# Where the preparation of w_out, the weights of FoX and the first loads of the output products stand in a hybrid decoder layer

## The chip, the cores and the metric

One core of a Trainium2 chip runs the program. The metric is device time in microseconds, from the first to the last instruction of the core and the little that lies around them; lower is better.

The engines are named as in the profile: PE (TensorE, with PEld for its weight loads), DVE (VectorE), ACT (ScalarE), POOL (GpSimd) and SP (SyncE), which issues all transfers here. SPq rows are issues of transfers. Each engine works through its instructions in order.

## The reference

A layer of a decoder: RMSNorm, one input projection, three mixers side by side (forgetting attention FoX with 8 heads of 64, gated linear attention GLA, a gated linear recurrence RG-LRU), each gated by silu, one output projection, RMSNorm, residual. 2048 frames and 16 meta tokens, width 1024.

```
hn   = rms_norm(h, pre_g)                      # (2176, 1024), the first 112 rows empty
proj = hn @ w_in                               # all mixers' columns
y    = concat(fox(...) * silu(fg), gla(...) * silu(gg), lru(...) * silu(lg)) * vmask   # width 2048
h    = h + rms_norm(y @ w_out, post_g)         # w_out: 2048 x 1024
return h[:, PAD:]

# FoX: c = cumsum(log_sigmoid(ff + b_f))
s = q.k / sqrt(64) + c[t] - c[s],  causal;   o = softmax(s) @ v
```

## The kernel before

Each float32 product is made of float16 products: a matrix is split into a high and a low half, scaled by a power of two that its sum of squares gives, and three products of halves are added. So every weight passes through a preparation: a load, a square with a sum on ACT, a column sum on PE, some small DVE operations for the scale, then the high half on ACT and the low half on DVE.

The work is a list of jobs (`hybrid_kernel`). Of each job its main part (`mix`) is written out step by step, and between its steps stand those of the next job's preparation (`prep`), which hold the input projections. The jobs are GLA's, then RG-LRU's, then FoX's sixteen. FoX goes by pairs of heads p = 0 to 3 and by chunks c = 0 to 3 of 512 queries; job (p, c) in this text is `fox_attend(k, p, c)`, beside which `fox_prepare` of the following (p, c) runs. A job has 4c + 5 steps, 176 in all.

One step of `fox_attend` takes 128 keys for both heads: eight matmuls into the double bank `sq` (line 1264), of which there is one; the exponential on ACT (line 1272) into `pt`; the sums `za` of the exponentials on DVE and, for one head of every second step, on POOL (line 1280); and two steps later four matmuls with the values (line 1288). At the end ACT copies the sums out (line 1294), and a chain of small transfers through DRAM (lines 503 to 510 and 1306) brings the reciprocals back. `fox_prepare` makes keys, queries, values and gate of its job and the row maxima: query-key products (line 1204), on DVE a maximum (line 1212), then a transposition, three small operations and six small transfers `QA<-dr` (line 1235), which the first step of the job needs.

`post` runs at the start of a job: it ends the conversions that are pending (`load_end`) and begins up to two weights of the list `todo`: `load_begin` issues the load and writes the square (line 454) at once. FoX's weights for pair p + 1 are begun in job (p, 1), keys and values, and in job (p, 3), queries and gate.

`wout_ready` prepares w_out during FoX: 32 blocks are loaded and squared (line 1338), three loads ahead; then in eight groups four blocks each are loaded again, four differences taken on POOL (line 1360), and seven pieces halved (`halves`, lines 1424 and 1425) and stored to DRAM (`wD`, line 1366): 56 halves. These are 95 steps of a generator; `merge` takes one of them behind each step of FoX from job (0, 0) on.

`project_out` then forms y @ w_out by blocks of two 128-row tiles (a pair), seven products of 24 matmuls each (line 1553). A pair's y is loaded (line 1437), squared (line 454 with `junk`), scaled and halved (lines 1468 to 1481, 1424, 1425). The prepared blocks come from `wD` into the memory of the normalised input `xhl` (four blocks, sixteen transfers) and into `ts` (three blocks). `out_begin` does the first pair's loads and halves and the blocks of `xhl` beside job (3, 3).

A scheduler puts the instructions into each engine's order by its own model of their durations. `tc.issue_after(i)` is the program's hold on it: what is written inside is queued behind instruction i on i's engine. `k.mark` and `k.store` name such instructions: the last store of y, of FoX or of w_out's pieces.

Of the kernel before, what the change touches and what calls it, by code (L numbers as in the profile page):

```python
# [11 lines left out]
BF16 = mybir.dt.bfloat16  # L12
# [62 lines left out]

OB = 8
GAP = 2
FA0 = (0, 0, 1, 3, 4, 5)  # L80
FA1 = (0, 0, 3, 5, 8, 9)
# [67 lines left out]
def drain(g):  # L149
    for _ in g:  # L150
        pass
# [15 lines left out]
def hybrid_kernel(tc, xT, x, w_grp, w_fa, vecs, w_a2, w_r, w_i, w_out, post_g, masks, out, yD=None):  # L167
    nc = tc.nc
    with ExitStack() as es:
# [40 lines left out]
        for t in range(8):  # L210
            for c in range(len(LP)):
                load = {}
                if t < 7:
                    load = {(t, 0): [("lx", t + 1), ("lg", t + 1)]}
                else:
                    load = {(7, 0): [("fk", 0), ("fv", 0)], (7, 2): [("fq", 0), ("fg", 0)]}
                flush = (5 * t + c) % 2 == 1
                prep, mix = lru_project(k, t, c), lru_mix(k, t, c, flush)
                if (t, c) == (0, 1):

                    w, prep0, mix0, n0, n_fill = jobs.pop()
                    jobs.append((w, chain(prep0, prep), chain(mix0, mix), n0 + 4, n_fill + 6))
                else:
                    jobs.append((load.get((t, c), []), prep, mix, 4 if flush else 3, 6))
        fox0 = len(jobs)
        for p in range(4):
            for c in range(NCH):
                load = {}
                if p < 3:
                    load = {1: [("fk", p + 1), ("fv", p + 1)], 3: [("fq", p + 1), ("fg", p + 1)]}  # L230
                jobs.append((load.get(c, []), fox_prepare(k, p, c), fox_attend(k, p, c), 4 * c + 5,
                             FILL[c] if (p, c) != (3, 3) else LAST_FILL))
        side = wout_ready(k)
        drain(jobs[0][1])
        for i, (_, _, mix, n_main, _) in enumerate(jobs):
            if i + 1 < len(jobs):
# [173 lines left out]
def load_begin(k, nm):  # L410
    load_dma(k, nm)
    load_squares(k)


def load_dma(k, nm):
    cols, src = (48, k.ins["w_fa"]) if nm == "fa" else (P, k.ins["w_grp"][GROUPS[nm]])
    raw = k.wp.tile([P, KT, P], F32, name="raw", bufs=RAWB)[:, :, 0:cols]
    with k.tc.issue_after(k.mark) if k.mark is not None else nullcontext():
        k.nc.sync.dma_start(out=raw, in_=src)
    k.sent.append((nm, raw, cols))  # L420

# [20 lines left out]
def post(k, n=1):  # L442

    while k.begun:
        load_end(k)
    for _ in range(min(n, len(k.todo))):
        load_begin(k, k.todo.pop(0))


def squares(k, tiles, scale=1.0):  # L450
# [446 lines left out]
        gla_keyed(k, 0, c1)  # L897


def beside(main, side, at):  # L900

    for i, _ in enumerate(main):
        for _ in range(at.count(i)):
            next(side, None)
        yield
# [266 lines left out]
def fox_prepare(k, p, c):  # L1172
# [59 lines left out]
    nc.vector.tensor_tensor(dr[:, 2, :], mr, dr[:, 1, :], op=ALU.subtract)  # L1232
    for h in range(2):
        for t in range(3):
            k.mark = nc.sync.dma_start(out=qx[64 * h + t:64 * h + t + 1, :].rearrange("o (i q) -> o i q", q=P),
                                       in_=dr[4 * h:4 * h + 4, t, :]).ins

    yield from rest
# [4 lines left out]
def fox_attend(k, p, c):  # L1243
# [8 lines left out]
    for j in range(nj):  # L1252
# [13 lines left out]
        if d >= 0:  # L1266
            v0 = NM if d == 0 else 0
            v1 = NM if d == 4 else P
            for h in range(2):
                nc.tensor.matmul(out=sp[0:m, h, off:off + v1 - v0], lhsT=k.identb[0:m, 0:m],  # L1270
                                 rhs=k.trib[0:m, v0:v1], start=False, stop=True)
        nc.scalar.activation(pt[0:m, :, off:], sp[0:m, :, off:], AF.Exp, scale=K.esc[0:m])  # L1272
        for h in range(2):
            if j == 1:
                if off:
# [42 lines left out]
def wout_ready(k):  # L1318
# [11 lines left out]
        return k.wk.tile([P, 2, KT // 2, P], F16, name="ws", tag="WS", bufs=BUFS["WS"])  # L1330

    order = [(q, b, j) for q in range(4) for b in range(4) for j in range(2)]
    raws = [load(*x) for x in order[0:3]]
    yield
    for i, (q, b, j) in enumerate(order):
        if b == j == 0:
            ss = small(k, "ssw", [P, 8], bufs=1)
        nc.scalar.activation(stage()[:, 0].bitcast(BF16), raws.pop(0), AF.Square, scale=2.0,
                             accum_out=ss[:, 2 * b + j:2 * b + j + 1])
        if i + 3 < len(order):  # L1340
            raws.append(load(*order[i + 3]))
        if (b, j) == (3, 1):
            yield
            nc.vector.tensor_reduce(ss[:, 0:1], ss, axis=AX.X, op=ALU.add)
            sc, inv = scale_of(k, ss[:, 0:1])
            for ring, x in ((k.wsc, sc), (k.winvs, inv)):
                ring.append(carve(k, 1))
                nc.vector.tensor_copy(ring[-1], x)
        yield
# [3 lines left out]
    for i, (q, j) in enumerate(groups):  # L1353
# [8 lines left out]

        def put(nm, x):
            hl = stage()
            halves(k, x, k.wsc[q], hl[:, 0], hl[:, 1])
            k.mark = nc.sync.dma_start(out=k.wD[BLOCKS.index(nm), :, j, :, q].rearrange(
                "z p k n -> p z k n"), in_=hl).ins

# [30 lines left out]
def out_begin(k):  # L1399

    nc = k.nc
    k.W = {}
    n = 4 * KT // 2 * P
    views = [[k.xhl[:, (4 * i + z) * n:(4 * i + z + 1) * n].rearrange("p (q k n) -> p q k n", q=4, n=P)
              for z in range(4)] for i in range(4)]
    k.winv = k.xhl[:, 16 * n:16 * n + 2 * CH].bitcast(F32)
    wout_load(k, BLOCKS[0], views[0])
    raws = pair_load(k, 0)
    for i in range(1, 4):
        k.load = wout_load(k, BLOCKS[i], views[i])  # L1410
    for q in range(4):
        nc.gpsimd.tensor_scalar(out=k.winv[:, P * q:P * q + P], in0=k.ones, scalar1=k.winvs[q], scalar2=None,
                                op0=ALU.mult)
    yield
    yield
    k.pairs = pair_halves(k, 0, raws)
    for _ in range(5):
        next(k.pairs)
        yield


# [10 lines left out]
def y_load(k, t):  # L1432
    yv = k.yD.rearrange("(h t p) n -> h p t n", p=P, h=2)
    raws = [tile4(k, "ZZ", "y") for _ in range(2)]
    for h in range(2):
        with k.tc.issue_after(k.store):
            k.load = k.nc.sync.dma_start(out=raws[h], in_=yv[h, :, :, P * t:P * t + P]).ins  # L1437
    return raws

# [184 lines left out]
```

## Time and profile before

| | |
|---|---|
| time, median of 3 runs | 2070.82 us (2068.61 to 2078.42) |
| profiled execution | 2072.19 us, span 2070.5 us |
| PE, DVE, ACT, POOL busy | 1918.2, 1284.5, 1011.7, 641.6 us |
| mean granted clock of PE | 0.968 |
| transferred | 152.70 MB |

The profile comes from one execution. Busy times add up over stages with different limits, so the stretches below are read one by one. A waiting time in brackets is the idle time of that engine just before the instruction, with what ended it. A granted clock of 1.00 is 2.4 GHz, 0.50 would be 1.2 GHz throughout; a number between them says in what share of the stretch each held.

### The profile page before, as it was taken

The numbers are of one execution on the slowest core, as the hardware profiler recorded it, in microseconds if no ns is written. First come the engines' busy times: TensorE is split into PE (matmuls) and PEld (weight loads), VectorE is DVE, ScalarE is ACT, GpSimd is POOL, SyncE is SP. The second block draws the span as 40 slices with busy tenths as digits, with TensorE's granted clock in tenths as the row PEclk, the third lists the DMA queues.
The fourth block names the chain that finished last, engine by engine and source line by source line (L and its number), as shares of the span: only waits on it lengthen the run. The fifth ranks groups of instructions, "written<-read, shape, count | busy, mean of one in ns | idle before, by whom it ended". The sixth has DMA issues, their size and how long they took to land. (4 is left out here: it accounts for less than half of the span.)

```text
span 2070.5 us, 39449 instructions
## 1 busy us (share of the span) xinstructions
PE 1918.2 (93%) x15988; PEld 990.9 (48%) x15988; DVE 1284.5 (62%) x2802; ACT 1011.7 (49%) x1561; POOL 641.6 (31%) x596
## 2 busy tenths in 40 slices
PE   6889999999899999999997989999999997899998
PEld 5455666665455555554333433354335432344443
DVE  6665453445777777754658867534753566487674
ACT  7645642345778888842445533322332235344441
POOL 3434233222333333321125621111211123253432
PEclk9889999999999999999998999999999998999999
DMA  6200120201111111111236640201020006843411
GB/s 220 68 7 28 40 84 27 72 23 51 57 41 41 41 46 42 62 51 29 67 100 205 207 127 12 72 13 32 18 66 12 12 12 234 242 141 96 135 58 61
DMA packets 116135, 152.70 MB, mean 74 GB/s; under 512 B 18792, under 2 KB 75816, under 8 KB 115952
## 3 DMA queue, kind: packets, MB, share of 16 engines
q1 hardware_dynamic: 115952, 150.18, 22.8%
q8 instruction: 125, 2.05, 0.4%
q14 instruction: 58, 0.48, 0.1%
HBM read 108.71 MB, written 41.33 MB: 72 GB/s over the span
## 5 line engine op out<-in xcount | busy, mean ns | idle before, releaser
L480 PE MATMUL pj<-xhl,whl 128*128 128x512 f16 (+3 forms) x3960 | 809.6, 356 | 9.1 <-ACT whl L437 4.2
L480 PEld LDWEIGHTS <-whl 128*128 128x128 f16 x3984 | 364.9, 98 | 391.2 <-issue 68.7
L1272 ACT ACTIVATE pt<-sq,consts 128x1024 f32<-128x1024 f32 (+4 forms) x176 | 163.1, 927 | 263.1 <-PE sq L1270 124.0
L1280 POOL TENSOR_TENSOR za<-za,pt 128x512 f32<-128x512 f32 (+1 forms) x80 | 98.6, 1233 | 540.5 <-ACT pt L1272 491.1
L1212 DVE CUSTOM_DVE_ANT_0 mj<-mq,CB 128x512 bf16<-128x512 f32 (+4 forms) x344 | 189.6, 580 | 69.0 <-PE mq L1204 35.8
L492 PEld LDWEIGHTS <-xhl 128*128 128x128 f16 (+1 forms) x3264 | 193.1, 100 | 35.5 <-issue 30.7
L1553 PEld LDWEIGHTS <-whl 128*128 128x128 f16 x1344 | 131.0, 98 | 164.4 <-issue 8.1
L492 PE MATMUL pj<-whl,xhl 128*128 128x128 f16 (+1 forms) x3024 | 198.1, 224 | 1.1 <-DVE consts L1212 1.1
L1280 DVE TENSOR_TENSOR za<-za,pt 128x512 f32<-128x512 f32 (+3 forms) x208 | 135.5, 675 | 92.0 <-ACT pt L1272 91.1
L1288 PE MATMUL fv<-pt,fv 128*64 128x512 f32 (+4 forms) x704 | 187.4, 549 | 2.1 <-ACT pt L1272 1.9
L1553 PE MATMUL pj<-xhl,whl 128*128 128x512 f16 x768 | 169.1, 380 | 0.0
L1264 PE MATMUL sq<-QA,KA 64*128 64x512 f16 (+4 forms) x1032 | 131.7, 351 | 18.7 <-ACT pt L1272 12.6
L1553 PE MATMUL pj<-ts,whl 128*128 128x512 f16 x576 | 127.9, 383 | 0.0
L558 DVE SCALAR_TENSOR_TENSOR xc<-lx,consts,xc 128x448 f32<-128x448 f32 (+1 forms) x120 | 98.9, 824 | 3.4
L1537 POOL TENSOR_TENSOR o<-o,xt 128x512 f32<-128x512 f32 x31 | 52.6, 1713 | 117.7 <-issue 60.6
L1264 PEld LDWEIGHTS <-KA 64*128 64x128 f16 (+1 forms) x1032 | 41.6, 95 | 95.1 <-issue 69.5
L1204 PE MATMUL mq<-KA,QA 64*128 64x512 f16 (+4 forms) x344 | 61.4, 345 | 21.8 <-DVE consts L1212 20.8
L516 ACT ACTIVATE gate<-pj,consts 128x512 f32<-128x512 f32 (+2 forms) x72 | 46.0, 640 | 72.7 <-PE pj L480 60.2
L1519 ACT ACTIVATE sqo<-o 128x512 bf16<-128x512 f32 x32 | 20.1, 629 | 123.4 <-DVE o L1513 123.4
L1559 DVE SCALAR_TENSOR_TENSOR o<-pj,consts,o 128x512 f32<-128x512 f32 x56 | 41.1, 745 | 59.1 <-PE pj L1553 54.8
L1264 PE MATMUL sq<-QA,KX 64*128 64x512 bf16 (+4 forms) x344 | 68.7, 351 | 3.9 <-DMA QA<-dr 3.9
L517 DVE SCALAR_TENSOR_TENSOR gate<-gate,pj 128x512 f32<-128x512 f32 (+2 forms) x72 | 45.2, 628 | 43.2 <-ACT gate L516 41.7
(253 smaller groups left out, 2832.6 us busy)
## 6 DMA issues: line engine op xcount, KB each, us to landing
raw<-in_w_grp_dram SPq DMA_DIRECT2D x44, 512.0 KB
wr<-in_w_out_dram SPq DMA_DIRECT2D x64, 256.0 KB
y<-yD SPq DMA_DIRECT2D x32, 512.0 KB
wD<-ws SPq DMA_DIRECT2D x56, 256.0 KB
CB<-c32D SPq DMA_DIRECT2D x32, 256.0 KB
xhl<-wD SPq DMA_DIRECT2D x16, 512.0 KB
xt<-in_x_dram SPq DMA_DIRECT2D x16, 512.0 KB
out_dram<-o SPq DMA_DIRECT2D x32, 256.0 KB
```

What stands on the lines that cost most here:

```text
L480: nc.tensor.matmul(out=ps, lhsT=a[:, kt, 0:m], rhs=b[:, kt, u0:u0 + n], start=i == 0, stop=i == 23)
L492: nc.tensor.matmul(out=ps, lhsT=a[:, kt, u0:u0 + m], rhs=b[:, kt, :], start=i == 0, stop=i == 23)
L516: k.act = nc.scalar.activation(out, ps, AF.Tanh, scale=hinv).ins
L558: nc.vector.scalar_tensor_tensor(out=xc, in0=lx[:, j:j + n], scalar=cw(j), in1=xc, op0=ALU.mult, op1=ALU.add)
L1204: nc.tensor.matmul(out=ps[:, h, 0:n], lhsT=qh[hs, P * i:P * i + P], rhs=d.hi[pc][hs, 0:n], start=True, stop=pc < c)
L1212: nc.vector.tensor_tensor_reduce(out=junk[:, h, 0:n], in0=ps[:, h, 0:n], in1=d.cb[pc][:, h, 0:n], scale=1.0, scalar=-3e38, op0=ALU.add, op ...
L1264: nc.tensor.matmul(out=sp[0:m, h, off:], lhsT=a[j // 4][hs, kk], rhs=b[hs, off:], start=i == 0, stop=i == 3 and d < 0)
L1272: nc.scalar.activation(pt[0:m, :, off:], sp[0:m, :, off:], AF.Exp, scale=K.esc[0:m])
L1280: eng.tensor_tensor(out=za[h][0:m, off:], in0=za[h][0:m, off:], in1=pt[0:m, h, off:], op=ALU.add)
L1288: nc.tensor.matmul(out=pv[hs, off1:], lhsT=V1[0:m1, j1 % 4, hs], rhs=pt1[0:m1, h, off1:], start=j1 == 0, stop=j1 == nj - 1)
L1537: eng.tensor_tensor(out=o, in0=o, in1=xt[:, h, :], op=ALU.add)
L1553: nc.tensor.matmul(out=ps, lhsT=a[:, kt, :], rhs=w[b + kt // 4][:, :, kt % 4, :], start=kt + j == 0, stop=(kt, j) == (KT - 1, 2))
```

## The change

- w_out's preparation: its 95 steps are spread over 150 of FoX's steps (`slowed`); its squares and the ACT part of its halves are queued behind the exponential written last (`k.exp`); its loads run six ahead.
- FoX's weights: the load and the square are two entries of `todo` now (`fox_loads`): keys and values are loaded in job (p, 0) and squared in (p, 1), queries and gate loaded in (p, 2) and squared in (p, 3); for pair 0 the same in RG-LRU's last jobs. Loads of other weights are no longer queued behind a store.
- The output: `out_begin` loads y of the first pair and then the blocks behind the last transfer of the maxima's rows (`k.dr`); later pairs' y is queued behind `k.mark`, not behind FoX's last store. The steps beside job (3, 3) are 16, nine of them empty, and the halves are queued behind exponentials.

The same instructions are issued; only their order differs.

```diff
-OB = 8
+OB = 16
+WOUT = (95, 150)
...
-                    load = {(7, 0): [("fk", 0), ("fv", 0)], (7, 2): [("fq", 0), ("fg", 0)]}
+                    load = {(7, c): x for c, x in fox_loads(0).items()}
...
-                load = {}
-                if p < 3:
-                    load = {1: [("fk", p + 1), ("fv", p + 1)], 3: [("fq", p + 1), ("fg", p + 1)]}
+                load = fox_loads(p + 1) if p < 3 else {}
...
-        side = wout_ready(k)
+        side = slowed(wout_ready(k), *WOUT)
...
 def load_dma(k, nm):
-    with k.tc.issue_after(k.mark) if k.mark is not None else nullcontext():
+    with k.tc.issue_after(k.mark) if nm[0] in ("fk", "fv", "fq", "fg") else nullcontext():
         k.nc.sync.dma_start(out=raw, in_=src)
...
     for _ in range(min(n, len(k.todo))):
-        load_begin(k, k.todo.pop(0))
+        nm = k.todo.pop(0)
+        if nm is None:
+            load_squares(k)
+        elif nm[0] == "load":
+            load_dma(k, nm[1])
+        else:
+            load_begin(k, nm)
+
+def fox_loads(p):
+    return {0: [("load", ("fk", p)), ("load", ("fv", p))], 1: [None, None],
+            2: [("load", ("fq", p)), ("load", ("fg", p))], 3: [None, None]}
...
+def slowed(g, n, of):
+    for i in range(of):
+        if (i + 1) * n // of > i * n // of:
+            next(g, None)
+        yield
+    drain(g)
...
-            k.mark = nc.sync.dma_start(out=qx[64 * h + t:64 * h + t + 1, :].rearrange("o (i q) -> o i q", q=P),
+            k.dr = k.mark = nc.sync.dma_start(out=qx[64 * h + t:64 * h + t + 1, :].rearrange("o (i q) -> o i q", q=P),
...
-        nc.scalar.activation(pt[0:m, :, off:], sp[0:m, :, off:], AF.Exp, scale=K.esc[0:m])
+        k.exp = nc.scalar.activation(pt[0:m, :, off:], sp[0:m, :, off:], AF.Exp, scale=K.esc[0:m]).ins
...
-    raws = [load(*x) for x in order[0:3]]
+    raws = [load(*x) for x in order[0:6]]
...
-        nc.scalar.activation(stage()[:, 0].bitcast(BF16), raws.pop(0), AF.Square, scale=2.0,
-                             accum_out=ss[:, 2 * b + j:2 * b + j + 1])
-        if i + 3 < len(order):
-            raws.append(load(*order[i + 3]))
+        with k.tc.issue_after(k.exp):
+            nc.scalar.activation(stage()[:, 0].bitcast(BF16), raws.pop(0), AF.Square, scale=2.0,
+                                 accum_out=ss[:, 2 * b + j:2 * b + j + 1])
+        if i + 6 < len(order):
+            raws.append(load(*order[i + 6]))
...
-            halves(k, x, k.wsc[q], hl[:, 0], hl[:, 1])
+            with k.tc.issue_after(k.exp):
+                halves(k, x, k.wsc[q], hl[:, 0], hl[:, 1])
...
 def out_begin(k):
+    k.mark = k.dr
...
-    wout_load(k, BLOCKS[0], views[0])
     raws = pair_load(k, 0)
-    for i in range(1, 4):
+    for i in range(4):
         k.load = wout_load(k, BLOCKS[i], views[i])
...
-    yield
-    yield
+    for _ in range(9):
+        yield
     k.pairs = pair_halves(k, 0, raws)
     for _ in range(5):
-        next(k.pairs)
+        with k.tc.issue_after(k.exp):
+            next(k.pairs)
         yield
...
-        with k.tc.issue_after(k.store):
+        with k.tc.issue_after(k.mark):
             k.load = k.nc.sync.dma_start(out=raws[h], in_=yv[h, :, :, P * t:P * t + P]).ins
```

Lines of the changed kernel have other numbers (the exponential 1272 is 1292, ACT's half 1424 is 1447, y's square 454 is 465, y's load 1437 is 1460). ACT in the middle of w_out's halves, before (`pt` is an exponential, `ws` a half, `fv` the values of the next job):

```order
L1424 ACTIVATE ws_13677<-wt_13506,consts_58 128x512
L1272 ACTIVATE pt_12968<-sq_12967,consts_58 128x1024
L1424 ACTIVATE ws_13776<-wt_13675,consts_58 128x512
L1424 ACTIVATE ws_13821<-wr_13044,consts_58 128x512
L1158 ACTIVATE fv_12816<-pj_12817,consts_58 128x512
L1424 ACTIVATE ws_13869<-wt_13774,consts_58 128x512
L1272 ACTIVATE pt_13024<-sq_13023,consts_58 128x1024
```

and where the halves begin after the change, in job (1, 2) instead of (0, 3):

```order
L1447 ACTIVATE ws_14309<-wr_14224,consts_58 128x512
L1292 ACTIVATE pt_14379<-sq_14378,consts_58 128x1024
L1447 ACTIVATE ws_14395<-wt_14307,consts_58 128x512
L1292 ACTIVATE pt_14414<-sq_14413,consts_58 128x1024
L1447 ACTIVATE ws_14428<-wr_14228,consts_58 128x512
L1292 ACTIVATE pt_14449<-sq_14448,consts_58 128x1024
L1292 ACTIVATE pt_14478<-sq_14477,consts_58 128x1024
```

Two or three halves between exponentials have become one or none. ACT in job (3, 3), before (`junk<-y` is y's square, `whl` its halves):

```order
L501 COPY zs<-fx 128x512
L1272 ACTIVATE pt<-sq,consts 128x1024 x5
L454 ACTIVATE junk,consts<-y 128x1024
L1272 ACTIVATE pt<-sq,consts 128x1024
L454 ACTIVATE junk,consts<-y 128x1024 x2
L1272 ACTIVATE pt<-sq,consts 128x1024
L454 ACTIVATE junk,consts<-y 128x1024
```

and after:

```order
L512 COPY zs<-fx 128x512
L1292 ACTIVATE pt<-sq,consts 128x1024 x10
L465 ACTIVATE junk,consts<-y 128x1024 x2
L1292 ACTIVATE pt<-sq,consts 128x1024
L465 ACTIVATE junk,consts<-y 128x1024 x2
L1292 ACTIVATE pt<-sq,consts 128x1024
```

The squares moved from behind the fifth exponential to behind the tenth. SP's queue at the start of job (3, 3), before (from the maxima's rows to the first blocks):

```order
L1235 DMA QA<-dr 1x4x128 x6
L503 DMA rowD<-zs 1x512 x2
L505 DMA consts<-rowD 128x8
L510 DMA rowD<-consts 128x8
L1306 DMA rz<-rowD 64x512 x2
L1308 DMA yD<-fo 128x512
L1437 DMA y<-yD 128x8x128 x4
L1394 DMA xhl<-wD 128x2048 x6
```

and after:

```order
L1255 DMA QA<-dr 1x4x128 x6
L1460 DMA y<-yD 128x8x128 x3
L514 DMA rowD<-zs 1x512 x2
L1460 DMA y<-yD 128x8x128
L1416 DMA xhl<-wD 128x2048
L516 DMA consts<-rowD 128x8
L1416 DMA xhl<-wD 128x2048 x2
L521 DMA rowD<-consts 128x8
```

Three of y's four loads now stand ahead of the whole normalisation of job (3, 2), and y's rest and the first blocks between its transfers.

## Rows read from the trace of the kernel before

**Rows 1.** Stretches: length; busy time of each engine; granted TensorE clock; DMA share; GB/s.

```profile
500.00:900.00 400.00, 384.28 (x2128) 220.70 (x2127) 305.40 (x537) 317.80 (x443) 152.99 (x187) 1.00 0.14 46
951.97:1152.80 200.83, 177.06 (x1205) 70.91 (x1204) 133.05 (x349) 90.37 (x153) 64.46 (x44) 0.94 0.36 116
951.97:1057.84 105.87, 98.78 (x663) 37.90 (x662) 63.43 (x207) 43.70 (x80) 17.90 (x15) 0.97 0.21 68
1152.80:1371.72 218.92, 201.12 (x1441) 86.41 (x1440) 142.37 (x356) 83.50 (x115) 63.28 (x49) 0.97 0.30 87
1399.41:1575.42 176.01, 168.16 (x1201) 68.39 (x1200) 97.10 (x293) 58.77 (x76) 31.93 (x25) 0.99 0.13 34
1399.41:1499.82 100.41, 95.89 (x658) 37.36 (x657) 62.17 (x191) 32.06 (x43) 17.53 (x14) 0.98 0.09 24
1399.41:1449.93 50.52, 47.79 (x338) 20.11 (x337) 24.56 (x79) 14.29 (x21) 7.29 (x6) 0.97 0.12 33
1603.10:1649.66 46.56, 46.45 (x338) 19.93 (x337) 24.18 (x76) 11.99 (x16) 7.27 (x6) 1.00 0.04 13
1698.37:1762.81 64.44, 49.76 (x268) 14.45 (x268) 40.45 (x60) 30.10 (x36) 23.38 (x14) 0.84 0.55 195
1762.81:1810.00 47.19, 39.85 (x178) 17.24 (x179) 17.93 (x26) 15.70 (x25) 11.59 (x5) 0.93 0.82 247
```

**Rows 2.** Line 1294: count, duration (min/median/max, ns), first and last start.

```profile
L1294 ACT COPY fo<-fv x16: 566/585/586, 952.0 to 1762.8; 128x512 f32<-128x512 f32 x16
```

**Rows 3.** Timeline of one step of job (3, 3).

```profile
1719.95 0.82 PE L1264 MATMUL sq<-QA,KA 64*128 64x512 f16 x6 [0.19 <-ACT pt L1272]
1720.59 0.39 PE L1264 MATMUL sq<-QA,KX 64*128 64x512 bf16 x2
1721.08 1.11 ACT L1272 ACTIVATE pt<-sq,consts 128x1024 f32<-128x1024 f32 x1 [1.18 <-PE sq L1264]
```

**Rows 4.** Lines of w_out's pieces; L1338 from 951.97 to 1057.84 only.

```profile
L1338 ACT ACTIVATE ws<-wr x19: 612/618/630, 986.2 to 1045.5; 128x512 bf16<-128x512 f32 x19
...
L1424 ACT ACTIVATE ws<-wt,consts x32: 705/712/724, 1101.5 to 1229.0; 128x512 f16<-128x512 f32 x32
...
L1425 DVE SCALAR_TENSOR_TENSOR ws<-wt,consts,ws x32: 732/752/1764, 1107.9 to 1230.3; 128x512 f16<-128x512 f32 x32
...
L1360 POOL TENSOR_TENSOR wt<-wr x16: 1257/1714/5558, 1097.4 to 1217.3; 128x512 f32<-128x512 f32 x16
```

**Rows 5.** ACT's waits, 900 to 1700: total us, times, longest.

```profile
ACT whl L454 <- DMA raw<-in_w_grp_dram: 23.9, 8, 4.4
```

**Rows 6.** Timeline, job (2, 1): start, us, engine, line, operation [idle before, releaser].

```profile
1431.00 1.06 ACT L454 ACTIVATE whl<-raw 128x1024 bf16<-128x1024 f32 x1 [3.76 <-DMA raw<-in_w_grp_dram]
1432.18 0.16 DVE L465 CAST consts<-consts 128x1 bf16<-128x1 f32 x1 [3.62 <-ACT whl L454]
1432.85 1.37 PE L1264 MATMUL sq<-QA,KA 64*128 64x512 f16 x6 [2.62 <-DVE consts L1212]
```

**Rows 7.** Timeline of SP's queue, the end of FoX.

```profile
1705.52 3.78 SPq L1235 DMA_DIRECT2D QA<-dr  x6
1721.18 4.51 SPq L1437 DMA_DIRECT2D y<-yD  x4
1783.24 11.17 SPq L1437 DMA_DIRECT2D y<-yD  x7
```

**Rows 8.** Timeline of ACT, job (3, 3).

```profile
1725.86 1.06 ACT L454 ACTIVATE junk<-y 128x1024 bf16<-128x1024 f32 x1 [3.67 <-DMA y<-yD]
1740.66 1.15 ACT L1424 ACTIVATE whl<-y,consts 128x1024 f16<-128x1024 f32 x1 [5.87 <-DVE consts L320]
```

**Rows 9.** Timeline of TensorE, job (3, 3) and behind.

```profile
1728.06 1.47 PE L1264 MATMUL sq<-QA,KA 64*128 64x512 f16 x6 [3.77 <-ACT pt L1272]
1738.72 0.25 PE L467 MATMUL mx<-consts 128*128 128x1 bf16 x4 [4.13 <-DVE consts L465]
1800.57 0.27 PE L467 MATMUL mx<-consts 128*128 128x1 bf16 x4 [7.34 <-DVE consts L465]
```

## The prediction

> **What bounds the kernel now.** I read the table of stretches first, because the chain that ended last is almost all matmuls of the output products and says little about the stage that the change touches. Its edges are the moments at which a FoX job (p, c) copies its sums out (line 1294, sixteen times) [rows 1, 2]. In each stretch the reader compares TensorE's busy time with the length: the difference is idle, and a granted clock under 1.00 is time at 1.2 instead of 2.4 GHz. Head pair 2's jobs 1 to 3 take 176.01 us with 7.9 idle at 0.99; the same jobs of pair 0 take 200.83 with 23.8 idle at 0.94; pair 1's four jobs take 218.92 with 17.8 idle at 0.97, pair 2's four (1371.72 to 1575.42) 203.70 [rows 1]. These three differ by w_out's preparation alone, which runs beside pairs 0 and 1. Pair 3's job 1, with neither w_out nor weights to load, takes 46.56 us with 0.1 idle; pair 2's job 1, which loads weights, 50.52 with 2.7 idle [rows 1]. The last job (64.44 us, 14.7 idle, clock 0.84) and what follows (47.19, 7.3 idle, 0.93) are the other poor stretches. So TensorE bounds the kernel, and what can be gained is its idle and half-speed time there.
>
> Then the timelines, to see who makes TensorE idle. In FoX's step a query-key product of eight matmuls (0.82 and 0.39 us) must follow the exponential that empties its bank (1.11 us on ACT), and the next exponential follows the product; ACT idles 1.18 us meanwhile [rows 3]. What stands on ACT behind an exponential costs nothing up to 1.2 us; what is above that is added to the step, unless TensorE has projection matmuls left.
>
> **w_out's preparation, 88 pieces on ACT.** Each of 32 squares takes 0.62 us there, each of 56 halves 0.71; a half also takes 0.75 on VectorE, and 32 of them (four in each of eight groups) need a subtraction of some 1.7 us on GpSimd [rows 4]. Nothing is removed; today they stand two, three or up to five between exponentials, later mostly one, queued behind an exponential, over 150 steps instead of 95 of 176. The present price is (200.83 - 176.01) + (218.92 - 203.70) = 40.0 us. Of it 5.5 (105.87 - 100.41) fall on the jobs with 19 squares [rows 1, 4], 0.29 each, though they stand four together; 40.0 - 5.5 = 34.5 over 56 halves is 0.62 each. After the change one piece of 0.62 or 0.71 fits into the 1.2 us, so ACT costs nothing; what remains is VectorE, which the maxima and the sums of FoX share. It is busy 97 of 176 us in the clean jobs, and 56 halves add 42 us (more where GpSimd interferes) spread over some 400. Bounds for a half are 0 and 0.62. I take 0.27, near the squares' 0.29, the nearest row with a single crowded engine: 56 x 0.27 = 15, and 1 for the squares: 16 remain, **24 gained** (bounds 0 to 40).
>
> VectorE's half takes 732 ns at least and 1764 at most; the longest is one subtraction's time above the shortest [rows 4]. The Trainium skill, "SBUF — State Buffer", section "Who interferes with whom", says that a VectorE instruction with two SBUF inputs and a GpSimd instruction that reads SBUF block one another for the whole instruction; the trace agrees in size. By that, spreading moves 32 such collisions beside more maxima of pairs 2 and 3 without making them fewer; the sum by the rule alone would keep the 40 us, and it is priced as two rivals below, from rows.
>
> The moved pieces bring their transfers along: w_out's loads (six ahead instead of three) and stores stand on SP's queue between FoX's small transfers. In the new order each store's VectorE half stands before the maxima's last operation, so no row of maxima waits for it; cost 0, else inside the bounds above.
>
> **FoX's weights.** ACT's square waited for its weights eight times, 23.9 us [rows 5]. The place in pair 2's job 1 shows the chain: square 3.76 us late, VectorE's cast behind it 3.62, TensorE 2.62 because the maxima stand behind that cast [rows 6]. A pair of loads costs 50.52 - 46.56 = 4.0 us, and six such pairs lie within FoX's jobs, 24 us. With the transfer issued a job (28 to 76 us) ahead the wait goes. Late next: two squares of 1.06 us between exponentials, 2.1 against 1.2, so 0.9 and some rest stay, say 1.5 per pair: **15 gained** (bounds 6 and 24). The loads pass the attention's small transfers on SP, and the four buffers are free then, since pending conversions are ended before new loads start. LRU's loads lose their place behind the y stores and move ahead; there TensorE is busy 384 of 400 us [rows 1] and covers them: 0, bounds -4 and +4, a quarter of its idle time there.
>
> **The last job.** y was issued at 1721.18, behind the normalisation of job (3, 2); its first square stood before the sixth exponential, waited 3.67 us, and TensorE idled 3.77; then 4.13 at the scale, the conversion on ACT 5.87 [rows 7 to 9]. Now y is issued right behind the maxima's row (its six small transfers are issued from 1705.52, 3.78 us long), about 11 us earlier, and squared after the tenth exponential, some 20 us after its issue. So these 7.9 us go. In their place: twice two squares, 2 x (2.1 - 1.2) = 1.8; then the scale and two conversions before an exponential, about 3: 4.8 back, 3.1 net. The clock of 0.84 is worth at most 10.3 us (0.16 x 64.44); with shorter gaps I count a fifth, 2.1. **5 gained** (bounds -5 and 14). The wait for the maxima's row itself, at the job's start, stays. GpSimd's sum and VectorE's difference of y now stand at the third step and hold their queues until y lands; their sums of exponentials run two or three buffers behind, which covers it. The normalisation of (3, 2) is overtaken by y and some blocks, but its result is read only by the fifth pair.
>
> **The second pair.** Its y was issued at 1783.24, behind the last store, though it reads rows of chunk 0 only; TensorE idled 7.34 us at 1800.57 [rows 7, 9], and the clock of 0.93 costs at most 0.07 x 47.19 = 3.3 [rows 1]. Now it follows the blocks, at about 1760, while the scale is wanted some four products later: **9 gained** (bounds 0 and 10.6).
>
> Sum: 24 + 15 + 5 + 9 = 53. The profiled execution took 2072.2 us (1.4 above the median of 2070.8): **2019 us**; its own range, with half of each term's distance to its bounds, 1999 to 2042.
>
> **Rivals.** (1) A half costs its 0.62 us wherever it stands, because VectorE and not ACT sets it; for it speaks that two engines are taken per half, against it that VectorE had 133 of 201 us in pair 0 and 97 of 176 in the clean jobs. The 24 are lost: 2043. (2) Everything hides: 40 + 24 + 14 + 10.6 = 88.6, 1984; for it pair 3's job 1 with 0.1 idle, against it that two squares still stand together. (3) SP's queue holds w_out's blocks: the small transfers of (3, 2), each waiting for another engine, now stand between them; for it the new order, against it that the second block is wanted only behind the last job. Both tail terms go: 2019 + 14 = 2033. (4) Slower: each half meets a subtraction at a place where TensorE waits for VectorE's maxima, in pairs 1 to 3 now. At the longest row, 1.76 us, 56 halves cost 98.6 instead of the 40; with 29 from the other terms, 2072.2 + 58.6 - 29 = 2102. It decides from (40 + 29) / 56 = 1.23 us per half, twice the present price; against it that the crowded place itself shows 0.62. That the change doesn't do what it says is excluded for the pieces: 95 of them fall on 150 of the 176 steps, and their end lies in job (3, 2), before the blocks are read.
>
> **How the numbers follow.** Forecast 0.60, rivals 0.17, 0.10, 0.07, 0.06. From 1998 to 2050 the range leaves out most of (2), the upper end of (1), and (4): under 0.2. A measurement here tells 0.5% (10 us) from no change. Faster than that: nearly all of the forecast, (2) and (3), and 0.85 of (1): 0.89; within it 0.04; slower 0.07.
>
> **What would show it.** Right: jobs 1 to 3 of pair 0 near 180 us and pair 1's four near 208, pairs 2 and 3 a few us longer than now, no ACT square waiting for weights, clock 1.00 through FoX; the first y at about 1710 on the old scale, no idle time at the second pair's scale. Wrong: idle before the maxima's products (line 1204) in pairs 2 and 3 in the tens of us (rivals 1 and 4), clock below 1.00 there, or output products that wait for xhl or ts (rival 3).

## The result and the profile after

The changed kernel takes 2018.12 us (median of 4 runs, 2013.52 to 2020.82) against 2070.41 of the kernel before (4 runs). The ratio is 0.9738, 95% interval 0.9706 to 0.9770; 2019 had been forecast. The profiled execution lasts 2016.83 us, span 2015.1, granted clock 0.976. The total agrees to 1 us, but not because every term did: RG-LRU gave 10.2 us that the forecast had at 0, and FoX and the second pair each gave about 5 us less than forecast.

First the stretches of the changed kernel, cut as in [rows 1, 2] at the copies of the sums (now line 1314). In order: pair 0's jobs 1 to 3, pair 1, job (1, 2) alone, pair 2, pair 3's jobs 0 to 2, the last job, the 47.19 us behind it. Columns as in [rows 1] (the five busy times are PE, PEld, DVE, ACT and POOL).

```profile
941.80:1115.72 173.92, 167.09 (x1203) 68.25 (x1202) 99.15 (x308) 69.94 (x116) 34.81 (x27) 0.99 0.20 62
1115.72:1322.49 206.77, 194.07 (x1443) 83.03 (x1442) 129.94 (x355) 80.95 (x119) 54.75 (x43) 0.98 0.25 75
1191.42:1249.77 58.35, 50.36 (x326) 18.01 (x325) 45.13 (x122) 23.74 (x32) 18.39 (x14) 0.94 0.27 87
1322.49:1530.01 207.52, 193.77 (x1441) 82.18 (x1440) 138.87 (x352) 83.03 (x115) 59.43 (x45) 0.99 0.28 88
1530.01:1654.25 124.24, 121.64 (x898) 51.65 (x897) 78.74 (x218) 41.65 (x59) 27.57 (x23) 1.00 0.12 40
1654.25:1711.65 57.40, 45.69 (x257) 13.86 (x256) 33.28 (x56) 30.34 (x36) 22.46 (x13) 0.88 0.74 261
1711.65:1758.84 47.19, 44.60 (x201) 19.37 (x200) 29.58 (x36) 17.89 (x27) 19.09 (x9) 0.96 0.72 213
```

Line 1314, as [rows 2]:

```profile
L1314 ACT COPY fo<-fv x16: 586/586/587, 941.8 to 1711.7; 128x512 f32<-128x512 f32 x16
```

Pair 0's three jobs became 26.9 us shorter, pair 1 12.2; pair 2 became 3.8 longer, pair 3's three jobs 1.3. The last job is 7.0 shorter, what follows it 4.2. And the first FoX job already ends 10.2 us earlier (941.8 for 952.0): that is RG-LRU, for which the forecast had 0.

Jobs (0, 1) to (3, 2) as one stretch, before and after:

```profile
951.97:1698.37 746.40, 694.96 (x4976) 291.63 (x4975) 451.55 (x1234) 274.76 (x400) 184.54 (x138) 0.97 0.22 68
941.80:1654.25 712.45, 676.57 (x4982) 285.11 (x4981) 446.70 (x1232) 275.56 (x407) 176.56 (x138) 0.99 0.23 69
```

Of the 34.0 us that went there, TensorE's idle time is 15.6 (35.9 for 51.4) and its busy time 18.4, at a granted clock of 0.990 for 0.973. Length times (1 - clock) is the most that 1.2 GHz can have cost: about 20 us before and 7 after. So the clock accounts for up to 13 us of the gain; it rose most in pair 0 (0.94 to 0.99), where TensorE's idle time fell most (23.8 to 6.8 us).

The lines of w_out's pieces, as [rows 4]: the same medians on ACT and VectorE within 0.01 us, GpSimd's 1.61 us for 1.71; they now run until 1626.9.

```profile
L1447 ACT ACTIVATE ws<-wt,consts x32: 705/711/722, 1227.1 to 1626.9; 128x512 f16<-128x512 f32 x32
...
L1448 DVE SCALAR_TENSOR_TENSOR ws<-wt,consts,ws x32: 737/752/1755, 1230.9 to 1627.9; 128x512 f16<-128x512 f32 x32
...
L1381 POOL TENSOR_TENSOR wt<-wr x16: 1261/1610/1719, 1225.8 to 1584.3; 128x512 f32<-128x512 f32 x16
```

ACT's wait for FoX's weights from 900 to 1700, as [rows 5]:

```profile
ACT whl L465 <- DMA raw<-in_w_grp_dram: 21.9, 8, 4.6
```

and the timeline of one of its places, in job (2, 2), as [rows 6] (SP, ACT and TensorE by time):

```profile
1434.39 0.86 SPq L418 DMA_DIRECT2D raw<-in_w_grp_dram  x2
1438.85 1.06 ACT L465 ACTIVATE whl<-raw 128x1024 bf16<-128x1024 f32 x1 [4.60 <-DMA raw<-in_w_grp_dram]
1441.05 0.82 PE L1284 MATMUL sq<-QA,KA 64*128 64x512 f16 x6 [3.63 <-ACT pt L1292]
```

The wait that the change was to end is still there (23.9 before). The square is written a job behind its load, but the load goes out in job (2, 2) and the square follows it there by 4.5 us: nothing holds the square to its job, and the scheduler put it into the job before, where it has to wait for its transfer.

The end, as [rows 7 to 9]: SP's queue, ACT's first y squares, the scales on TensorE.

```profile
1660.51 3.90 SPq L1255 DMA_DIRECT2D QA<-dr  x6
1664.45 2.34 SPq L1460 DMA_DIRECT2D y<-yD  x3
...
1711.64 1.00 SPq L1460 DMA_DIRECT2D y<-yD  x2
...
1689.75 1.05 ACT L465 ACTIVATE junk<-y 128x1024 bf16<-128x1024 f32 x1
...
1697.30 0.24 PE L478 MATMUL mx<-consts 128*128 128x1 bf16 x4 [2.14 <-DVE consts L476]
...
1715.16 1.99 PE L1319 MATMUL fx<-za,consts 128*64 128x512 f32 x4 [2.59 <-DVE za L1300]
1735.51 0.24 PE L478 MATMUL mx<-consts 128*128 128x1 bf16 x4
```

y is issued 10.2 us behind job (3, 2)'s copy (22.8 before) and squared without a wait; the second pair's scale has no idle time in front of it (7.34 before), but a new gap of 2.59 stands at the sums of the last job.

### The profile page after: what moved, and what is told of

Same layout as the page of the kernel before. It is cut to its first block, busy times and chain, and to the rows that moved or that the text cites. A ratio compares the mean times of both kernels' runs of the same rounds, so it can differ in the third digit from the quotient of the medians.

```text
span 2015.1 us, 39446 instructions
## 1 busy us (share of the span) xinstructions
PE 1893.3 (94%) x15988; PEld 985.4 (49%) x15988; DVE 1265.8 (63%) x2802; ACT 1011.9 (50%) x1561; POOL 630.7 (31%) x596
## 4 chain that ended last, share of the span: by engine, by line
PE 66%; DVE 8%; DMA 5%; ACT 5%; issue 4%; POOL 4%; SPq 1%; POOLq 0%; ACTq 0%; DVEq 0%
PE pj L491 26%; PE pj L1576 14%; PE pj L503 5%; PE fv L1308 5%; PE sq L1284 4%; PE mq L1224 2%; DMA raw<-in_w_grp_dram 2%; PE st L596 1%; DMA rz<-rowD 1%; DVE mj L1232 1%; PE gs L1034 1%; DMA rowD<-consts 1%; PE pv L1068 1%; DVE xc L569 1%; POOL v L618 1%
## 5 line engine op out<-in xcount | busy, mean ns | idle before, releaser
L1308 PE MATMUL fv<-pt,fv 128*64 128x512 f32 (+4 forms) x704 | 174.7, 534 | 0.6 <-DVE QA L1106 0.6
L569 DVE SCALAR_TENSOR_TENSOR xc<-lx,consts,xc 128x448 f32<-128x448 f32 (+1 forms) x120 | 94.0, 783 | 3.5
L1542 ACT ACTIVATE sqo<-o 128x512 bf16<-128x512 f32 x32 | 20.1, 630 | 129.5 <-DVE o L1536 129.5
L604 POOL TENSOR_TENSOR v<-a 128x448 f32<-128x448 f32 (+1 forms) x40 | 39.0, 976 | 134.1 <-ACT a L602 134.1
```

Source lines behind the costliest of these rows:

```text
L569: nc.vector.scalar_tensor_tensor(out=xc, in0=lx[:, j:j + n], scalar=cw(j), in1=xc, op0=ALU.mult, op1=ALU.add)
L1308: nc.tensor.matmul(out=pv[hs, off1:], lhsT=V1[0:m1, j1 % 4, hs], rhs=pt1[0:m1, h, off1:], start=j1 == 0, stop=j1 == nj - 1)
```

## The experiments

The runs come from different chips, so each ratio is to runs of the kernel before on the same chip. This table has the lengths of the stretches in the profiled executions, from the sixteen starts of the copy of the sums in each (first job's end, pair 0's jobs 1 to 3, pair 1, pair 2, pair 3's jobs 0 to 2, last job, rest). Gains are given either by the ratio or as a difference of profiled spans ("by the spans"); the latter are single executions, most of them on different chips, and a few us of such a difference mean little.

| kernel | to (0,0) | pair 0 | pair 1 | pair 2 | pair 3 | (3,3) | rest |
|---|---|---|---|---|---|---|---|
| before | 951.97 | 200.83 | 218.92 | 203.70 | 122.95 | 64.44 | 307.69 |
| changed | 941.80 | 173.92 | 206.77 | 207.52 | 124.24 | 57.40 | 303.45 |
| LRU alone (b_lru) | 940.64 | 199.06 | 220.22 | 203.74 | 122.96 | 64.27 | 307.41 |
| weights alone (b_fox) | 954.60 | 191.82 | 215.00 | 198.32 | 122.96 | 64.44 | 304.36 |
| w_out alone (b_wout) | 952.56 | 181.00 | 216.91 | 224.59 | 125.06 | 62.41 | 303.97 |
| end alone (b_out) | 950.07 | 200.87 | 222.04 | 204.37 | 122.95 | 60.76 | 310.54 |
| changed, weights undone (a_nofox) | 941.99 | 180.49 | 215.06 | 225.86 | 127.58 | 54.74 | 305.78 |
| changed, w_out undone (a_nowout) | 945.53 | 191.07 | 213.70 | 198.21 | 122.96 | 57.59 | 303.34 |
| changed, end undone (a_noout) | 943.91 | 172.19 | 204.98 | 208.18 | 124.56 | 62.86 | 306.92 |
| changed, squares held (a_hold) | 941.54 | 168.94 | 201.80 | 202.43 | 124.01 | 55.44 | 305.54 |
| weights alone, held (b_hold) | 958.68 | 191.51 | 207.98 | 197.60 | 122.96 | 66.18 | 303.79 |
| held, w_out undone (h_nowout) | 945.78 | 191.31 | 205.48 | 197.58 | 122.91 | 56.82 | 303.52 |
| held, no queueing (h_free) | 942.06 | 180.30 | 225.81 | 199.48 | 122.89 | 56.01 | 305.75 |
| held, other plan (h_plan) | 942.08 | 167.11 | 202.42 | 205.63 | 130.90 | 55.64 | 303.42 |

**Each part alone.** Four kernels, each the kernel before with one part of the change; `b_lru` is

```diff
-    with k.tc.issue_after(k.mark) if k.mark is not None else nullcontext():
+    with k.tc.issue_after(k.mark) if nm[0] in ("fk", "fv", "fq", "fg") else nullcontext():
```

> The kernel before with one thing of the change alone: LRU's weight loads (lx, lg) are no longer queued behind the last store of y; FoX's loads stay as they were, squared in the job that loads them. Theory of the prediction: TensorE's projections cover these loads, 0 us (-4 to +4), 2070. Rival, from the profile of the changed kernel, whose first FoX job ends 10.2 us earlier (941.8 for 952.0): LRU's weights were what it lost there, 9 to 12 us faster, about 2060, and the first FoX job ends near 942.

Measured 2056.98, ratio 0.9935 (0.9916 to 0.9954); the first FoX job ends at 940.64. The rival holds: the whole of RG-LRU's gain comes from this one condition. ACT's wait for those weights between 500 and 890 us, in the kernel before and in this one:

```profile
ACT whl L454 <- DMA raw<-in_w_grp_dram: 11.0, 9, 3.4
```

```profile
ACT whl L454 <- DMA raw<-in_w_grp_dram: 1.6, 2, 1.4
```

Over the same matmuls of this stage (459.8 to 861.5 us before, 460.1 to 849.0 here) the kernel takes 388.9 us for 401.7. TensorE's idle time there is 8.6 us for 17.1, and its busy time 380.3 for 384.6, at a clock of 1.00 in both.

`b_fox`: `fox_loads` with the new `post`, the old condition on all loads.

```diff
-                    load = {1: [("fk", p + 1), ("fv", p + 1)], 3: [("fq", p + 1), ("fg", p + 1)]}
+                load = fox_loads(p + 1) if p < 3 else {}
```

> The kernel before with FoX's weight loads posted a job ahead of their squares, and nothing else (all loads still queued behind the last store). Theory of the prediction: the wait of the squares for their transfer goes, 15 us faster, 2055. Rival, from the changed kernel, whose squares still wait 21.9 us for the transfer: the square is not held back to its job, it stands 3 to 4 us behind its load as before, so the wait stays and only its place moves: 0 us (-3 to +3), 2070, with ACT's wait for raw near 22 us between 900 and 1700.

Measured 2054.58, ratio 0.9930 (0.9903 to 0.9957): the size of the prediction, in part by another way. ACT still waits 18.8 us for raw, in 6 places. A wait of TensorE went. In the kernel before, job (0, 3):

```profile
1090.53 1.06 ACT L454 ACTIVATE whl<-raw 128x1024 bf16<-128x1024 f32 x1 [4.39 <-DMA raw<-in_w_grp_dram]
...
1091.92 0.16 PE L467 MATMUL mx<-consts 128*128 128x1 bf16 x1 [4.91 <-DVE consts L465]
```

Queries and gate are needed in the very job that loaded them, so their scale product stood in TensorE's queue right behind the square and stopped everything behind it. Between 900 and 1700 TensorE waited 12.9 us at scale products, in 5 places; 10.1 in 4 places are these weights', the fifth (2.81 us at 1036.97) is the scale of a group of w_out's blocks. With loads and squares a job earlier the weights' scale products come 30 us or more behind the squares, and 0.3 us of the 12.9 are left. Jobs (0, 3), (1, 3) and (2, 3) are 6.1, 6.8 and 3.7 us shorter.

That is not the whole account. Job (2, 1), where keys and values were loaded, is 3.9 us shorter too (46.57 us, like pair 3's job without loads), though ACT's wait has only moved into job (2, 0). There it costs nothing (27.79 us for 27.69), since TensorE has projection matmuls at that moment:

```profile
1380.02 1.06 ACT L464 ACTIVATE whl<-raw 128x1024 bf16<-128x1024 f32 x1 [2.64 <-DMA raw<-in_w_grp_dram]
1380.89 1.51 PE L502 MATMUL pj<-whl,xhl 128*128 128x128 f16 x24
```

At two other new places it costs more: jobs (1, 0) and (2, 2) are 4.2 and 2.2 us longer.

`b_wout`: the new `wout_ready` (`issue_after(k.exp)` around squares and halves, six loads ahead) and

```diff
-        side = wout_ready(k)
+        side = slowed(wout_ready(k), *WOUT)
```

> The kernel before with w_out's preparation spread over 150 steps, queued behind the exponentials and six blocks ahead; weights, y and the output blocks as they were. Theory of the prediction: 24 us faster (16 of the 40 remain), 2046. Rival: the weights' term was empty and the preparation gave FoX's whole 34 us, 2036. By the second rival of the prediction (all is hidden) 40, 2030.

Measured 2067.99, ratio 0.9997 (0.9978 to 1.0016): nothing, which no theory had said. Pair 0 is 19.8 us shorter and pair 2 20.9 longer. Job (2, 3) of this kernel (SP, ACT, TensorE):

```profile
1518.25 0.33 SPq L1318 DMA_DIRECT2D yD<-fo  x1
1518.62 0.92 SPq L420 DMA_DIRECT2D raw<-in_w_grp_dram  x2
...
1523.38 1.06 ACT L455 ACTIVATE whl<-raw 128x1024 bf16<-128x1024 f32 x1 [7.31 <-issue]
...
1524.77 0.16 PE L468 MATMUL mx<-consts 128*128 128x1 bf16 x1 [7.21 <-DVE consts L466]
```

The load still stands behind the store of the previous job's output, and ACT's square and TensorE's scale product, placed early in the job, wait for it 7.3 and 7.2 us each (the profile names no releaser for this square; for the one in job (1, 3), 7.43 us, it names the load); in job (1, 3) 7.4 and 7.3. The scale product's wait explains only part of the 14.4 us by which job (2, 3) is longer. The job before and here:

```profile
1499.82:1575.42 75.60, 72.26 (x544) 31.03 (x543) 34.93 (x103) 26.71 (x34) 14.40 (x11) 1.00 0.19 48
1485.02:1575.06 90.04, 77.34 (x535) 32.71 (x532) 49.00 (x120) 32.64 (x43) 22.78 (x19) 0.89 0.34 98
```

TensorE is idle 12.7 us for 3.3, 4.7 of the difference at the scale product (7.21 for 2.48). Its busy time is 5.1 us longer, at a clock of 0.89 for 1.00; the longest stretch at 1.2 GHz is 1520.1 to 1533.8 us, from the standstill on. The other 6.5 us of pair 2's 20.9 lie in jobs (2, 0) to (2, 2).

`b_out`: the new `out_begin`, `pair_load` and OB, nothing else.

```diff
-        with k.tc.issue_after(k.store):
+        with k.tc.issue_after(k.mark):
             k.load = k.nc.sync.dma_start(out=raws[h], in_=yv[h, :, :, P * t:P * t + P]).ins
```

> The kernel before with the end alone changed: the first pair's y issued behind the maxima's row and squared after the tenth exponential of the last job, its blocks and the second pair's y behind it. Theory of the prediction: 5 in the last job and 9 at the second pair, 14 us faster, 2056. Rival, from the changed kernel (57.4 us for 64.4 in the last job, 303.5 for 307.7 behind it): 11 us, 2059, the second pair's gap gone but most of it given back later. If the exponentials' queue carries the squares badly without the rest of the change: 2070.

Measured 2071.08, ratio 1.0014 (0.9997 to 1.0032). SP's queue shows why it says little on the mechanism:

```profile
1726.64 0.32 SPq L1308 DMA_DIRECT2D yD<-fo  x1
1727.01 4.94 SPq L1438 DMA_DIRECT2D y<-yD  x4
...
1782.09 0.33 SPq L1308 DMA_DIRECT2D yD<-fo  x1
1782.45 9.62 SPq L1438 DMA_DIRECT2D y<-yD  x7
```

Both y loads stayed behind the stores of FoX's output. `issue_after` only sets the earliest place, and here the scheduler chose late ones. So this run prices neither of the two terms.

**Each part taken out of the changed kernel.** `a_nofox` puts back the loads and squares in jobs 1 and 3 (and RG-LRU's (7, 0) and (7, 2)):

```diff
-                load = fox_loads(p + 1) if p < 3 else {}
+                load = {}
+                if p < 3:
+                    load = {1: [("fk", p + 1), ("fv", p + 1)], 3: [("fq", p + 1), ("fg", p + 1)]}
```

> The changed kernel with FoX's weights loaded and squared in one job again, as before. If the parts' terms are independent, as the prediction summed them (measured alone: weights 14.5 us): 2032. Rival, from the spread preparation alone, where pair 2 took 224.6 us for 203.7 because ACT stood 5 to 7 us at the weights' squares: each of the two parts needs the other, and without the weights' part pair 2 loses 17 us, pair 1 some 10 and pair 0 some 7: 2050.

Measured 2050.93 (before 2067.49), ratio 0.9932 (0.9909 to 0.9954), as the rival said. TensorE waits 7.47 us in job (1, 3) and 7.61 in (2, 3) at the scale product:

```profile
1288.21 0.16 PE L480 MATMUL mx<-consts 128*128 128x1 bf16 x1 [7.47 <-DVE consts L478]
...
1514.51 0.16 PE L480 MATMUL mx<-consts 128*128 128x1 bf16 x1 [7.61 <-DVE consts L478]
```

`a_nowout` has `wout_ready` of the kernel before and

```diff
-        side = slowed(wout_ready(k), *WOUT)
+        side = wout_ready(k)
```

> The changed kernel with w_out's preparation as before (95 steps, one piece a step, three blocks ahead, not queued behind exponentials). If independent (measured alone: 0): 2018. By the prediction's term: 24 more, 2042. Rival, parts that need each other: FoX as with the weights' part alone, pair 0 192, pair 1 215, pair 2 198: 16 more, 2034.

Measured 2033.73, ratio 0.9848 (0.9815 to 0.9881): the rival, parts that need each other.

`a_noout` has `out_begin`, `pair_load` and OB of the kernel before.

```diff
-OB = 16
+OB = 8
```

> The changed kernel with the end as before (y behind the last normalisations, the second pair's y behind the last store). By the prediction's terms 14 more, 2032; by the profile of the changed kernel 11, 2029; if as in the end's change alone: 0, 2018.

Measured 2025.92, ratio 0.9811 (0.9779 to 0.9844): 8.5 us by the spans (2023.6 and 2015.1), 5.5 of it in the last job and 3.5 behind it.

**The wait that stayed.** `a_hold` queues the weights' squares behind the exponential that was written last when their job began ("held" in the table):

```diff
         if nm is None:
-            load_squares(k)
+            with k.tc.issue_after(k.exp) if getattr(k, "exp", None) else nullcontext():
+                load_squares(k)
```

> The changed kernel with the weights' squares also queued behind the exponential that was the last one traced when their job began, so that they really stand a job (some 25 to 50 us) behind their transfers. In the changed kernel they stand 3 to 5 us behind them and ACT waits 21.9 us. Theory: that wait is on the path (TensorE idled 3.0 and 3.6 us at two of the places); 10 to 16 us faster, 2005, ACT's wait for raw near 0. Rival: TensorE's projections and the maxima cover it, or the conversion comes late for the next job's projections: 2013 to 2022.

Measured 2003.15 (2000.48 to 2008.56; before 2067.49), ratio 0.9706 (0.9664 to 0.9747). ACT has no wait for raw in FoX; around (2, 2)'s end the load and square now stand 20 us apart:

```profile
1420.71 0.37 SPq L418 DMA_DIRECT2D raw<-in_w_grp_dram  x1
...
1440.34 1.06 ACT L466 ACTIVATE whl<-raw 128x1024 bf16<-128x1024 f32 x1
```

This is the better kernel by the profiled span (1999.7 for 2015.1) and by the medians. The two ratios do not come from the same chip and their intervals overlap.

`b_hold` is `b_fox` with the same edit on top.

> The kernel before with FoX's weights loaded a job ahead and their squares held back behind the job's exponentials, so that they really stand a job behind the transfer; nothing else. Measured so far: without the hold 14.5 us faster, though ACT's wait for the transfer stayed (18.8 us); the hold on top of the changed kernel 15 more. If the two add here too: 25 to 30 us faster, 2040, ACT's wait for raw gone. If the hold only helps beside the spread preparation: 14.5, 2053.

Measured 2052.14, ratio 0.9935 (0.9915 to 0.9954): no better than `b_fox` in time. FoX's jobs from (0, 1) to (3, 2) are 8 us shorter than there (pair 1 by 7.0), but the first job ends 4 us later and the last job is 1.7 longer. Why RG-LRU's end moved is not settled.

**The preparation by itself.** `h_nowout` is `a_hold` with the edit of `a_nowout` on top.

> The changed kernel with the weights' squares held back, and w_out's preparation as before. Where the weights no longer wait, this prices the preparation by itself: theory of the prediction, 24 us of 40: 2027 for 2003. Rival: it is worth what the changed kernel showed without the hold (2033.7 for about 2015, 18 us), 2021; second rival: the hold and the spread work on the same idle time, under 10 us, 2012.

Measured 2028.06, ratio 0.9817 (0.9796 to 0.9839); by the spans 23.7 us slower than `a_hold`. That is the prediction's 24 in sum, once the weights are out of the way, but not in its parts. In this kernel pair 2 (197.58 us, its last three jobs 169.75) carries neither pieces nor waits for weights; against it pair 0 is 21.6 us longer and pair 1 7.9, so the preparation costs 29.5 us and not the 40.0 of the prediction. In `a_hold` pieces cost 9.4 us, not 16. That is 20.1 us between jobs (0, 1) and (3, 2); 4.2 more lie before the first job's end, where the forecast had nothing. Of the 20.1 TensorE's idle time is 9.6 and its busy time 10.5, at a clock of 0.998 for 0.988.

`h_free` is `a_hold` without the edge on w_out's squares (likewise) and halves:

```diff
-            with k.tc.issue_after(k.exp):
-                halves(k, x, k.wsc[q], hl[:, 0], hl[:, 1])
+            halves(k, x, k.wsc[q], hl[:, 0], hl[:, 1])
```

> The changed kernel with the weights' squares held back, w_out's pieces spread over 150 steps and loaded six ahead, but their ACT instructions not queued behind the exponentials. If the spreading alone is what helps: 2003. If a piece in front of an exponential costs its 0.6 to 0.7 us at most of 88 places, up to 55 us lost: between 2010 and 2035; 2015 taken, since the pieces then mostly stand in the gap anyway.

Measured 2033.04, ratio 0.9841 (0.9819 to 0.9863), 33 us slower than `a_hold` by the spans, the upper end of what was expected. But the expectation took the spreading as kept, and without the edge there is none: the halves end at 1355 us, not at 1612 as in `a_hold`, though the code spreads them over the same 150 steps. So this run does not price a piece in front of an exponential by itself:

```profile
L1446 ACT ACTIVATE ws<-wt,consts x32: 708/712/726, 1230.5 to 1355.2; 128x512 f16<-128x512 f32 x32
```

`h_plan` is `a_hold` with steps given job by job, none in (1, 2), (2, 2) and (3, 2), and pair 0's weights unqueued.

```diff
-WOUT = (95, 150)
+WOUT = ((38, 58), (0, 13), (16, 17), (4, 5), (8, 9), (0, 13), (16, 17), (4, 5), (9, 9))
```

> A version meant to beat both: the changed kernel with the squares held back, pair 0's weights not queued behind the store of y, and w_out's halves kept out of the third job of each pair (where TensorE idles 1.9 to 6.2 us and VectorE is busy 44 of 51 to 55 us), denser in the other three. Theory: 3 us in LRU and up to 7 in the third jobs, against 2 to 4 where the halves stand denser: 1997, 3.4% faster than before. Rival: VectorE's crowding only moves to the fourth jobs: 2003.

Measured 2008.23, ratio 0.9721 (0.9703 to 0.9740): not better than `a_hold`, and RG-LRU gave none of the 3 us. Against `a_hold`, jobs (0, 2) and (1, 2) are 2.8 and 3.0 us shorter, (1, 3) and (2, 3) 3.6 and 2.9 longer, and (3, 1) 7.0 longer, where VectorE carries nine halves beside the maxima (five in `a_hold`) and TensorE waits at one place 3.73 us:

```profile
1550.33 0.34 PE L1226 MATMUL mq<-KA,QA 64*128 64x400 f16 x2 [3.73 <-DVE consts L1234]
```

## Why the prediction was right, and where it was not

**The total** held, 2019 for 2018, and to that precision by luck. Against the profiled 55.4 us: RG-LRU gave 10.2 (forecast 0), FoX up to (3, 2) 34.0 (39), the last job 7.0 (5), the rest 4.2 (9). The first error makes up for the second and the fourth. (Half the distances to the slow bounds are 12, 4.5, 2, 5 and 4.5 us, so the prediction's own range should have ended at 2047, not 2042.)

**The step that failed**, in the prediction's words: "With the transfer issued a job (28 to 76 us) ahead the wait goes." It did not go (21.9 of 23.9 us). The distance was read off the job in which load and square are written; where the scheduler put them, the square follows its load by 4.5 us. The part was still worth 14.5 us alone: ACT's wait stayed but moved, for pair 2's keys and values to a place where TensorE has work, and TensorE's own wait at the scale products of queries and gate went, which the prediction doesn't name. The hold shows what the step would have been worth beside the spread: 15.4 us more by the spans.

**RG-LRU's loads** were priced at nothing in the words "there TensorE is busy 384 of 400 us [rows 1] and covers them". A share of 96% did not exclude 10 us: the step failed at using a busy share as a cover, and its bound of 4 us, a quarter of the idle time, was too narrow. `b_lru` took half of TensorE's idle time there (8.4 of 17.1 us) and 4.4 us of its busy time. The wait that the prediction had in front of it was ACT's 11.0 us in 9 places.

**The sum of the terms** was wrong as a form. By the ratios the kernel's time changes by -13.4, -14.5, -0.6 and +2.9 us with each of the four parts alone, -26 together and not -54. The spread preparation is worth 0 beside the old weights, 17.3 us in the changed kernel and 23.7 with the weights held (by spans). The prediction priced the spread by its own pieces and did not ask which other wait the new order would make longer: TensorE's for the weights' scale, 7.3 and 7.2 us in jobs (1, 3) and (2, 3) where it had been 2.5 in each. And it read the difference between the pairs as "w_out's preparation alone"; of the 40.0 us only 29.5 are that, by `h_nowout`. Why the same squares and halves cost 20.9 us more in pair 2 beside the old weights is shown only in part (the scale product and the clock of job (2, 3)).

**A half's price.** Forecast 0.27. In the changed kernel itself it is 0.34: against pair 2 and pair 3 of `a_nowout` its pairs 1 to 3 are 8.6, 9.3 and 1.3 us longer, over 56 halves. With weights held, `a_hold` against pair 2 and pair 3 of `h_nowout`, which have no pieces: pair 1 4.2, pair 2 4.9, pair 3 1.1 us over 56 halves, 0.18 each. For the old places `h_nowout` gives 0.40: its 29.5 us less 7.0 that its jobs (0, 1) and (0, 2), with the squares, are longer than (2, 1) and (2, 2). Pair 0's squares cost nothing in `a_hold` (168.94 us; the clean three jobs of pair 2 in `h_nowout` take 169.75). So rival (1), 0.62 wherever, and rival (4), above 1.23, are out. So is rival (2): even with the weights held 2003 remain, not 1984. Rival (3) is out: no output product waits for xhl or ts.

The Trainium skill, "SBUF — State Buffer", section "Who interferes with whom", would keep the collisions of VectorE and GpSimd as many as they were. The traces agree for the change itself: of the 56 VectorE halves 19 take over 0.9 us before and 20 after, all of them beside a GpSimd instruction, and together they take 56.6 and 55.5 us. From `h_nowout` to `a_hold` they do fall, from 24 to 18 and from 61.7 to 54.2 us, while a half's price fell from 0.40 to 0.18. That it matters whether TensorE waits for VectorE at that moment would fit this, but no run separates it. One reading of the prediction is off: the longest half is 1.03 us above the shortest, and a subtraction takes 1.26 us at least [rows 4], so the excess is less than one subtraction.

**What would show it**: pair 1 at 206.77 (near 208) and pairs 2 and 3 at +3.8 and +1.3 were right, as were the first y (about 1709 on the old scale) and the second pair's scale. Pair 0 did better (173.92, not 180). Wrong was "no ACT square waiting for weights". Of the signs against it, the idle time before the maxima's products is 5.0 us in pair 2 and 2.5 in pair 3 (1.9 in each before), not tens. The clock did not reach 1.00 throughout: 0.94 in job (1, 2), where the first halves and a pair of waiting squares meet.

**The end**: the last job's term was a little small. The second pair's 9 was mis-sized by half: its gap of 7.34 went, but y's halves now stand on VectorE ahead of the last sums, and TensorE waits 2.59 us there:

```profile
1712.25 1.27 DVE L1448 SCALAR_TENSOR_TENSOR whl<-s,consts,whl 128x1024 f16<-128x1024 f32 x1
1713.45 1.66 DVE L1300 TENSOR_TENSOR za<-za,pt 128x144 f32<-128x144 f32 x3
```

Beside the rest of the change, `a_noout` prices the two terms at 5.5 and 3.5 us, for 5 and 9 forecast.

## What to carry to other kernels

When a change moves a load ahead of its use, look in each engine's order for the distance between the two. A job in the code is no distance where a scheduler may pull the use forward; here an edge on the using engine's queue kept it. Price a late transfer by the in-order engine that stands behind it and is the bound, not by the wait that the profile names first. Compare busy time and granted clock of the bound engine too, not its waits alone. And do not add the terms of parts that share one queue: here one part was worth 0 without the other, 17 us with it, and 24 when the other was held in place.

## What the runs showed that was not expected

With TensorE busy 96% of a stretch [rows 1], the kernel still became 10 us faster when ACT's wait of 11.0 us for its weights shrank to 1.6; TensorE's busy time itself fell by 4.4 us at the same clock. Spacing VectorE's halves three times wider (400 us for 127) left the number of slowed ones at 20 of 56, from 19. And of the 34 us gained in FoX more than half is shorter busy time of TensorE, at a higher clock, and not idle time.
